# FFN gate and up projections: one 512-column matmul for the upper weight part, halves added when PSUM is read

## The chip, the cores and the metric

The kernel runs on one core of a Trainium2 chip. The metric is the device time of one execution in microseconds (us); the number given for a kernel is the median of its runs. All data are float32; a matmul operand is tagged float32r.

## What is computed

Two layers of a hybrid trunk act on x of 256 tokens by 1024 channels. Each layer is an FFN, a block of three token mixers, and a second FFN, each followed by a residual and a LayerNorm. The change touches the FFNs alone; there are four of them.

```python
D_MODEL = 1024
SEQ = 256
DEPTH = 2
D_FF = 2816

def _swiglu(x, w_in, w_out):
    gate, up = jnp.split(x @ w_in, 2, axis=-1)
    return (jax.nn.silu(gate) * up) @ w_out

def reference(...):
    for l in range(DEPTH):
        x = _layernorm(DEEPNORM_ALPHA * x + FFN_RES * _swiglu(x, ffn1_w_in[l], ffn1_w_out[l]),
                       ln1_g[l], ln1_b[l])
        mix = _hybrid_mixer(x, l, ...)
        x = _layernorm(DEEPNORM_ALPHA * x + mix, ln2_g[l], ln2_b[l])
        x = _layernorm(DEEPNORM_ALPHA * x + FFN_RES * _swiglu(x, ffn2_w_in[l], ffn2_w_out[l]),
                       ln3_g[l], ln3_b[l])
    return x
```

## The kernel before

**Split products.** Every float32 operand of a matmul is held as two parts: an upper part (hi, a copy rounded to float32r) and a lower part (lo, what is left). A product a·b is three matmuls into the same PSUM region, hi·hi, hi·lo and lo·hi (`passes`, line 124). Weights come from HBM by SP's queue into `raw` (`wraw`, 2 buffers of 1 MB; `rawo` for the output weights); ScalarE makes `whi` (L93) and VectorE subtracts to make `wlo` (L94), in pieces of 128x1024 out of the pool `wsp`, which has 6 buffers of each. `split_act` (L128, L129) does the same to activations. In the trace PE names the stationary operand second: `gm<-xThi,whi` has weights `whi` loaded and `xThi` streamed through.

**Activations.** `new_xT` allots two tiles of 128 x (8·256 + 128) elements, `xThi` and `xTlo`, and uses 8·256 columns of each from column `APART` = 48 (192 bytes) on. `transposed` fills them after each LayerNorm (L145, L128, L129). Both the FFNs and the mixers read them.

**One FFN** (`ffn`, line 236) walks over 11 blocks of 256 hidden channels, j = 0 to 10.
- Block 0 is done by `part_a` with tokens as output rows (L275), so that it can begin with the first half of the tokens while the second half still goes through the LayerNorm before.
- Blocks 1 to 10 are done by `part_s`: two weight loads (gate and up, 1 MB each), then `gemm_s` (L135) four times: gate f=0 and f=1 into the two halves of one PSUM tile `pg`, up f=0 and f=1 into those of `pu`. A `gemm_s` is 8 steps k of three matmuls, each with 256 columns of x streamed. ScalarE applies Silu to `pg` (L297), VectorE multiplies by `pu` (L300), and `split_act` makes `hhi` and `hlo`.
- `out_mm` (L308) multiplies h of block j−2 (`LAG` = 2) by its output weights, 24 matmuls of 512 columns into four PSUM accumulators that stay open for the whole FFN. The second token half of the last three blocks is held back (`HOLD` = 3) to cover the LayerNorm of the first half.

**PSUM.** The pools `gm` and `tp` have two banks each, `at` has four. `pg` and `pu` are the two `gm` banks; `tp` serves transposes.

**Order.** Each engine runs its instructions in the order in which a scheduler that simulates the program wrote them down; an engine waits where the next one in its list is not ready.

**Mixers.** Between the FFNs stand projections of the same split kind: `block_s`, `gate` and `proj` through `gemm_s` (also L135, 256 columns), `block_a` (L368, 512 columns of weights streamed, x loaded as the stationary operand), and `mix_out` (L730).

Of the kernel before, what the change touches and what calls it, by code (L numbers as in the profile page):

```python
# [11 lines left out]
F32 = mybir.dt.float32  # L12
F32R = mybir.dt.float32r
BF16 = mybir.dt.bfloat16
AF = mybir.ActivationFunctionType
# [5 lines left out]
P = 128  # L21
D = 1024
S = 256
L = 2
FF = 2816
KT = D // P
# [4 lines left out]
HOLD = 3  # L31

APART = 48
OFF_QA, OFF_KA, OFF_VA, OFF_ZB, OFF_XBC, OFF_DTB, OFF_QC, OFF_KC, OFF_VC, OFF_G = (
    0, 1024, 2048, 3072, 4096, 5632, 5648, 6672, 7696, 8720)
NEG = -float(2 ** 100)
# [4 lines left out]
def hybrid_trunk(ctx: ExitStack, tc: tile.TileContext, x, ffn1_w_in, ffn1_w_out, ln1_g, ln1_b,  # L41
# [4 lines left out]
    pe, act, dve, pool = nc.tensor, nc.scalar, nc.vector, nc.gpsimd  # L46

    const = ctx.enter_context(tc.tile_pool(name="const", bufs=1))
    keep = ctx.enter_context(tc.tile_pool(name="keep", bufs=1))
# [8 lines left out]
    def gm_tile():  # L58
        return gm.tile([P, 512], F32, name="gm")

    def tp_tile():
        return tp.tile([P, 512], F32, name="tp")
# [48 lines left out]
    def load_cols(w, c0, between=None, raw=None):  # L111
        return load(w, 0, 8, c0, 256, None, between, raw)
# [4 lines left out]
    def load_block(w, c0):  # L117
        return load_half(w, 0, c0) + load_half(w, 4, c0)
# [5 lines left out]
    def passes(a, b):  # L124
        return ((a[0], b[0]), (a[0], b[1]), (a[1], b[0]))

    def split_act(hi, lo, src):
        act.copy(out=hi, in_=src)  # L128
        dve.tensor_sub(out=lo, in0=src, in1=hi.bitcast(F32))  # L129

    def gemm_s(ps_out, w, f, xT, n=P):
        first = True
        for k in range(KT):
            for i, (a, b) in enumerate(passes(w[k], xT)):
                pe.matmul(out=ps_out, lhsT=a[:, f:f + n], rhs=b[:, k, :],  # L135
                          start=first, stop=(k == KT - 1 and i == 2))
                first = False


    def transposed(t, xT):  # L140
        for q in range(2):
            pt = tp_tile()
            for i in range(4):
                k = 4 * q + i
                pe.transpose(out=pt[:, i * P:(i + 1) * P], in_=xt[:, t, k * P:(k + 1) * P], identity=ident)  # L145
            pv = pt.rearrange("p (k c) -> p k c", c=P)
            split_act(xT[0][:, 4 * q:4 * q + 4, t * P:(t + 1) * P], xT[1][:, 4 * q:4 * q + 4, t * P:(t + 1) * P], pv)

    def new_xT():
        def part(name):  # L150
            whole = keep.tile([P, KT * S + 128], F32R, name=name)
            return whole[:, APART:APART + KT * S].rearrange("p (k c) -> p k c", c=S)

        return part("xThi"), part("xTlo")

    def layernorm(t, accs, coef, gb, sq):
        st = sm.tile([P, 5], F32, name="st")
# [78 lines left out]
    def ffn(xT, w_in, w_out, g, b, l, pre, prefetch, fresh=False, last=False, tiles_a=1):  # L236
        NJ = FF // 256
        with tc.tile_pool(name="ffn", bufs=2, reuse_waits="tile") as fp:
# [7 lines left out]
            def new_h():  # L246
                return (fp.tile([P, 2, S], F32R, name="hhi", bufs=5), fp.tile([P, 2, S], F32R, name="hlo", bufs=5))
# [40 lines left out]
            def part_s(j):  # L288
                spare = fresh and j == 1
                wg = load_cols(w_in[l], j * 256, None, raws[0] if spare else None)  # L290
                wu = load_cols(w_in[l], FF + j * 256, None, raws[1] if spare else None)
                pg, pu = gm_tile(), gm_tile()
                hT = new_h()
                for f in range(2):
                    gemm_s(pg[:, f * S:(f + 1) * S], wg, f * P, xT)
                sg = fp.tile([P, 512], F32, name="h")
                act.activation(out=sg, in_=pg, func=AF.Silu)  # L297
                for f in range(2):
                    gemm_s(pu[:, f * S:(f + 1) * S], wu, f * P, xT)
                dve.tensor_mul(out=sg, in0=sg, in1=pu)  # L300
                split_act(hT[0], hT[1], sg.rearrange("p (f c) -> p f c", c=S))
                return hT

# [10 lines left out]
            for j in range(tiles_a, NJ + LAG):  # L314
                if j < NJ:
                    hs[j] = part_s(j)
                pj = j - LAG
                if pj < 0:
                    continue
                if pj < NJ - HOLD:  # L320
                    wo = load_rows(w_out[l], 2 * pj, None, raws[pj] if pj < 2 and not fresh else new_raw())
                    for t in range(NT):
                        out_mm(pj, hs[pj], wo, t)
                else:
                    wo = load_rows(w_out[l], 2 * pj, held_pair(), new_raw())
                    if pj < NJ - 1:
                        out_mm(pj, hs[pj], wo, 0)
                    else:
                        pre2 = prefetch and prefetch()
                        for h in range(2):  # L330
                            out_mm(pj, hs[pj], wo, 0, (h,))
                    held.append((pj, wo))
                if pj == NJ // 2:
                    load_gb(gb, g, b, l)
                if fresh and pj == 2:
                    consts.append(mixer_constants())
            for t in range(NT):
                if t == 1:
                    for h in range(2):
                        for pj, wo in held:  # L340
                            out_mm(pj, hs[pj], wo, 1, (h,))
                layernorm(t, accs[t], 0.5, gb, sq)
                if last:
                    for h in range(2):
                        nc.sync.dma_start(out=out_v[:, t, 512 * h:512 * h + 512], in_=xt[:, t, 512 * h:512 * h + 512])
                else:
                    if xT2 is None:
                        xT2 = new_xT()
                    transposed(t, xT2)
# [3 lines left out]
    def mixer(xT, l, pre, prefetch, consts):  # L353
# [4 lines left out]
        with tc.tile_pool(name="mix", bufs=1, reuse_waits="tile") as mp:  # L358
            def slot(tag, shape, dt=F32):
                return mp.tile(shape, dt, name=tag, tag=tag)  # L360
# [17 lines left out]

            ss = mp.tile([P, APART], F32, name="ss")[:, 0:2 * 8].rearrange("p (t h) -> p t h", h=8)
            zs = slot("t1", [P, NT, D])  # L380
# [383 lines left out]
            for t in range(NT):  # L764
                if t == 1:
                    for h in range(2):
                        for q in (1, 2, 3):
                            mix_out(q, wo[q], t, (h,))
                layernorm(t, accs[t], 0.5, gb, slot("xde", [P, D]))
                if xT2 is None:  # L770
                    xT2 = new_xT()
                transposed(t, xT2)
        return xT2, pre2

    def ffn_first(w_in, l, between=None):
        return lambda: (load_cols(w_in[l], 0, between), load_cols(w_in[l], FF))

    xT = new_xT()
    consts = []
    pre = ffn_first(ffn1_w_in, 0, lambda: load_x(0, 1))()  # L780
    for l in range(L):
        xT, pre = ffn(xT, ffn1_w_in, ffn1_w_out, ln1_g, ln1_b, l, pre, lambda: load_block(w_mix_in[l], OFF_ZB),
                      fresh=(l == 0))
        xT, pre = mixer(xT, l, pre, ffn_first(ffn2_w_in, l), consts[0])
        last = l == L - 1
        xT, pre = ffn(xT, ffn2_w_in, ffn2_w_out, ln3_g, ln3_b, l, pre, None if last else ffn_first(ffn1_w_in, l + 1), last=last)
# [37 lines left out]
```

## Time and profile before

| | us |
|---|---|
| median of 3 runs | 1610.74 |
| lowest and highest run | 1610.71, 1612.2 |
| the profiled execution, its own time | 1617.37 |
| its span, first to last instruction | 1615.6 |
| TensorE (PE) busy in the span | 1591.5 (99%) |
| VectorE (DVE) busy | 984.7 (61%) |
| ScalarE (ACT) busy | 848.4 (53%) |
| mean granted TensorE clock, share of full speed | 0.994 |

PE's busy time does not say how fast it goes: matmuls overlap, and a row's duration (282 ns for a 256-column one) is longer than the distance from its start to the next one's start. How long a stretch of matmuls takes is read from the chain of work that ended last, which lists stretches of one engine and one line with start, length and count. The profiled execution took 6.63 us more than the median of the runs; sums are made on its rows and carried over as differences.

### The profile page before, as it was taken

Reading aid. Unit: us, or ns where it says so; the run is one execution under the profiler, and the core shown is the slowest. Engines: PE = TensorE matmul, PEld = TensorE weight load, DVE = VectorE, ACT = ScalarE, POOL = GpSimd, SP = SyncE. Lnnn points to the kernel's source line nnn. Section 1 sums busy time; section 2 is a strip of 40 time slices with the busy share of each in tenths; the row PEclk is TensorE's granted clock in tenths of the full one; section 3 lists DMA queues with packets and bytes.
Section 4 is the critical chain, followed back from the end, with each engine's and each line's share of the span. In section 5 each row is a group of like instructions: output and inputs, shape, how many; then the busy total and the mean of one; then the engine's idle time right before and its main releaser. Section 6 shows DMA issues by size and latency. Waiting matters only on the chain.

```text
span 1615.6 us, 26930 instructions
## 1 busy us (share of the span) xinstructions
PE 1591.5 (99%) x11282; PEld 1467.2 (91%) x11282; DVE 984.7 (61%) x1510; ACT 848.4 (53%) x1285; POOL 17.6 (1%) x28
## 2 busy tenths in 40 slices
PE   8999999999999999999999999999999999999998
PEld 8999899888799998999899998998788999999997
DVE  5555657767585556455655565777576855565454
ACT  5545356568675444444444453654676755444451
POOL 0000000000000000000000000000000000000000
PEclk9999999999999999999999999998999999999999
DMA  8665445543435674566445562663443356545651
GB/s 286 198 226 192 158 157 175 187 161 105 157 106 174 217 235 140 175 216 225 157 162 203 209 230 85 208 190 128 154 140 124 129 194 216 191 157 183 235 196 39
DMA packets 222117, 283.55 MB, mean 176 GB/s; under 512 B 8658, under 2 KB 185644, under 8 KB 221996
## 3 DMA queue, kind: packets, MB, share of 16 engines
q1 hardware_dynamic: 213676, 277.61, 51.0%
q10 hardware_dynamic: 8320, 4.23, 0.9%
q8 instruction: 88, 1.44, 0.4%
q14 instruction: 33, 0.27, 0.0%
HBM read 280.74 MB, written 1.08 MB: 174 GB/s over the span
## 4 chain that ended last, share of the span: by engine, by line
PE 95%; DVE 2%; DMA 2%; ACT 1%; issue 0%; POOL 0%; DVEq 0%; POOLq 0%; ACTq 0%
PE gm L135 52%; PE at L308 15%; PE gm L368 14%; PE gm L275 3%; PE at L730 2%; DMA t<-acd 2%; PE at L633 1%; PE at L507 1%; PE at L585 1%; PE at L577 1%; PE at L555 1%; PE tp L614 0%; DVE wlo L94 0%; DVE at L169 0%; DVE xt L160 0%; PE tp L145 0%
## 5 line engine op out<-in xcount | busy, mean ns | idle before, releaser
L94 DVE TENSOR_TENSOR wlo<-raw,whi 128x1024 fp32r<-128x1024 f32 x412 | 501.2, 1223 | 360.5 <-ACT whi L93 350.4
L93 ACT CAST whi<-raw 128x1024 fp32r<-128x1024 f32 x412 | 429.4, 1051 | 391.0 <-PE gm L135 229.4
L135 PE MATMUL gm<-xThi,whi 128*128 128x256 f32 x2112 | 595.1, 282 | 0.0
L135 PE MATMUL gm<-xTlo,whi 128*128 128x256 f32 x2112 | 594.8, 282 | 0.0
L135 PE MATMUL gm<-xThi,wlo 128*128 128x256 f32 x2112 | 594.2, 281 | 0.0
L135 PEld LDWEIGHTS gm<-xThi,wlo 128*128 128x128 f32 x2112 | 403.8, 191 | 1.8 <-issue 1.8
L135 PEld LDWEIGHTS gm<-xThi,whi 128*128 128x128 f32 x2112 | 398.4, 189 | 3.4 <-issue 1.8
L135 PEld LDWEIGHTS gm<-xTlo,whi 128*128 128x128 f32 x2112 | 397.9, 188 | 3.0 <-issue 1.6
L135 PE MATMUL gm<-t,whi 128*128 128x256 f32 x768 | 138.7, 282 | 0.0
L368 PE MATMUL gm<-whi,xThi 128*128 128x512 f32 x320 | 128.7, 402 | 1.2 <-ACT xThi L128 1.2
L94 DVE TENSOR_TENSOR wlo<-rawo,whi 128x1024 fp32r<-128x1024 f32 x68 | 83.1, 1225 | 72.8 <-ACT whi L93 69.7
L368 PE MATMUL gm<-whi,xTlo 128*128 128x512 f32 x320 | 126.9, 398 | 0.0
L368 PE MATMUL gm<-wlo,xThi 128*128 128x512 f32 x320 | 126.4, 395 | 0.0
L135 PEld LDWEIGHTS gm<-t,whi 128*128 128x128 f32 x768 | 117.2, 188 | 2.7 <-issue 2.7
L93 ACT CAST whi<-rawo 128x1024 fp32r<-128x1024 f32 x68 | 71.3, 1052 | 76.8 <-PE at L308 63.7
L135 PE MATMUL gm<-t,wlo 128*128 128x256 f32 x384 | 108.1, 281 | 0.0
L308 PE MATMUL at<-whi,hhi 128*128 128x512 f32 x256 | 78.9, 390 | 0.0
L308 PE MATMUL at<-wlo,hhi 128*128 128x512 f32 x256 | 78.9, 390 | 0.0
L308 PE MATMUL at<-whi,hlo 128*128 128x512 f32 x256 | 78.9, 390 | 0.0
L135 PEld LDWEIGHTS gm<-t,wlo 128*128 128x128 f32 x384 | 73.1, 190 | 0.0
L368 PEld LDWEIGHTS gm<-whi,xThi 128*128 128x128 f32 x320 | 60.3, 188 | 13.9 <-ACT xThi L128 2.1
L368 PEld LDWEIGHTS gm<-whi,xTlo 128*128 128x128 f32 x320 | 60.2, 188 | 13.5 <-DVE xTlo L129 0.9
(235 smaller groups left out, 1870.5 us busy)
## 6 DMA issues: line engine op xcount, KB each, us to landing
raw<-in_w_mix_in_dram SPq DMA_DIRECT2D x92, 1024.0 KB, 5.1
raw<-in_ffn_w_in_dram SPq DMA_DIRECT2D x85, 1024.0 KB, 4.9
rawo<-in_ffn_w_out_dram SPq DMA_DIRECT2D x44, 1024.0 KB, 7.2
raw<-in_w_branch_dram SPq DMA_DIRECT2D x24, 1024.0 KB, 5.5
raw<-in_w_mix_out_dram SPq DMA_DIRECT2D x8, 1024.0 KB, 6.2
t<-acd ACTq DMA_DIRECT2D x4, 1024.0 KB
rawo<-in_ffn_w_in_dram SPq DMA_DIRECT2D x2, 1024.0 KB
gb<-in_ln_g_dram SPq DMA_DIRECT2D x4, 512.0 KB
```

The lines of the kernel that those rows point to most:

```text
L93: act.copy(out=hi, in_=src)
L94: dve.tensor_sub(out=lo, in0=src, in1=hi.bitcast(F32))
L135: pe.matmul(out=ps_out, lhsT=a[:, f:f + n], rhs=b[:, k, :], start=first, stop=(k == KT - 1 and i == 2))
L275: pe.matmul(out=ps[:, u * 256:(u + 1) * 256], lhsT=a[:, k, t * P:(t + 1) * P], rhs=c, start=first, stop=(k == KT - 1 and i == 2))
L308: pe.matmul(out=accs[t][h], lhsT=a[:, f, t * P:(t + 1) * P], rhs=c[:, h * 512:(h + 1) * 512], start=(j == 0 and f == 0 and i == 0), stop=( ...
L368: pe.matmul(out=ps, lhsT=a[:, k, t * P:(t + 1) * P], rhs=c, start=(k == 0 and i == 0), stop=(k == KT - 1 and i == 2))
L507: pe.matmul(out=py[:, 64 * h:64 * h + 64], lhsT=m[:, hh, :], rhs=xdt[:, c, 64 * hh:64 * hh + 64], start=True, stop=True)
L555: pe.matmul(out=pz[h][:, 0:S], lhsT=kcT[r, hp, 0:P], rhs=qcT[r, hp, :], start=True, stop=False, skip_group_check=True)
L577: pe.matmul(out=pz[h][:, 0:384], lhsT=trin, rhs=part[:, hs], start=False, stop=False, skip_group_check=True)
L585: pe.matmul(out=pz[c0][64 * h:64 * h + 64, 384:512], lhsT=vct[:, k, 64 * hh:64 * hh + 64], rhs=sp[:, 384 * h + c1:384 * h + c1 + P], start ...
L633: pe.matmul(out=pm[m][:, c:c + n], lhsT=qaT[r, h, t * P:(t + 1) * P], rhs=kaT[r, h, 0:n], start=True, stop=True, skip_group_check=True)
L730: pe.matmul(out=accs[t][h], lhsT=a[:, k, t * P:(t + 1) * P], rhs=c[:, h * 512:(h + 1) * 512], start=(k == 0 and i == 0), stop=(k == KT - 1 ...
```

## The change

- `new_xT` allots one tile of 128 x (8·512 + 128) elements. For each k it holds 256 columns of the upper part and, right behind, 256 of the lower one. It returns the two parts as before (now strided) and, as a third item, the whole with 512 columns per k. The data begin at column `XPART` = 48, 192 bytes.
- `gemm_j` takes the place of `gemm_s` in `part_s`. For each k it issues one matmul of 512 columns (upper weights by both parts of x) and one of 256 (lower weights by the upper part of x, added to columns 0 to 255). Three matmuls and three weight loads per k become two and two.
- The result of one f fills a whole PSUM bank: columns 256 to 511 hold hi·lo, columns 0 to 255 the rest. ScalarE copies the upper half to SBUF and VectorE adds the lower half to it, for each of the four products of a block. Silu and the multiplication then read SBUF. Gate uses the two `gm` banks, up the two `tp` banks.
- The mixers and `part_a` keep their instructions and read x from the new places.

```diff
+XPART = 48
...
+    def gemm_j(w, f, xT, ps):
+        for k in range(KT):
+            pe.matmul(out=ps, lhsT=w[k][0][:, f:f + P], rhs=xT[2][:, k, :], start=(k == 0), stop=(k == KT - 1),
+                      skip_group_check=True)
+            pe.matmul(out=ps[:, 0:S], lhsT=w[k][1][:, f:f + P], rhs=xT[0][:, k, :], start=False, stop=(k == KT - 1),
+                      skip_group_check=True)
+        return ps
...
     def new_xT():
-        def part(name):
-            whole = keep.tile([P, KT * S + 128], F32R, name=name)
-            return whole[:, APART:APART + KT * S].rearrange("p (k c) -> p k c", c=S)
-
-        return part("xThi"), part("xTlo")
+        whole = keep.tile([P, KT * 2 * S + 128], F32R, name="xTj")[:, XPART:XPART + KT * 2 * S]
+        both = whole.rearrange("p (k i c) -> p k i c", i=2, c=S)
+        return both[:, :, 0, :], both[:, :, 1, :], whole.rearrange("p (k c) -> p k c", c=2 * S)
...
-                pg, pu = gm_tile(), gm_tile()
                 hT = new_h()
+                sg = fp.tile([P, 512], F32, name="h")
                 for f in range(2):
-                    gemm_s(pg[:, f * S:(f + 1) * S], wg, f * P, xT)
-                sg = fp.tile([P, 512], F32, name="h")
-                act.activation(out=sg, in_=pg, func=AF.Silu)
+                    ps = gemm_j(wg, f * P, xT, gm_tile())
+                    sf = sg[:, f * S:(f + 1) * S]
+                    act.copy(out=sf, in_=ps[:, S:2 * S])
+                    dve.tensor_add(out=sf, in0=sf, in1=ps[:, 0:S])
+                act.activation(out=sg, in_=sg, func=AF.Silu)
+                su = fp.tile([P, 512], F32, name="h")
                 for f in range(2):
-                    gemm_s(pu[:, f * S:(f + 1) * S], wu, f * P, xT)
-                dve.tensor_mul(out=sg, in0=sg, in1=pu)
+                    ps = gemm_j(wu, f * P, xT, tp_tile())
+                    sf = su[:, f * S:(f + 1) * S]
+                    act.copy(out=sf, in_=ps[:, S:2 * S])
+                    dve.tensor_add(out=sf, in0=sf, in1=ps[:, 0:S])
+                dve.tensor_mul(out=sg, in0=sg, in1=su)
```

How the instructions move is shown at three places. **First, PE inside a gate block.** In the kernel before, two steps k of one product read as follows; `gm` is the PSUM tile.

```order
L135 MATMUL gm<-xThi,whi 128x256
L135 MATMUL gm<-xTlo,whi 128x256
L135 MATMUL gm<-xThi,wlo 128x256
L135 MATMUL gm<-xThi,whi 128x256
L135 MATMUL gm<-xTlo,whi 128x256
L135 MATMUL gm<-xThi,wlo 128x256
```

In the changed kernel the same work on PE is the following, where `xTj` is the joint tile; L143 and L145 are the two matmuls of `gemm_j`.

```order
L143 MATMUL gm<-xTj,whi 128x512
L145 MATMUL gm<-xTj,wlo 128x256
L143 MATMUL gm<-xTj,whi 128x512
L145 MATMUL gm<-xTj,wlo 128x256
L143 MATMUL gm<-xTj,whi 128x512
```

Sixty-four such matmuls stand where 96 stood in each of the blocks 1 to 10, and the 24 of `out_mm` follow them as before.

**Second, ScalarE over one block of the first FFN.** Before, its list has one Silu from PSUM (L297), the upper parts of six weight pieces (L93) and that of h (L128).

```order
L93 CAST whi<-raw 128x1024 x2
L297 ACTIVATE h<-gm 128x512
L93 CAST whi<-raw 128x1024 x2
L128 CAST hhi<-h 128x512
L93 CAST whi<-rawo 128x1024 x2
```

In the changed kernel four copies from PSUM are among them (L305 for gate, L312 for up; L95, L130 and L307 are the casts and the Silu).

```order
L305 COPY h<-gm 128x256
L95 CAST whi<-raw 128x1024 x2
L305 COPY h<-gm 128x256
L312 COPY h<-tp 128x256
L307 ACTIVATE h<-h 128x512
L95 CAST whi<-raw 128x1024 x2
L312 COPY h<-tp 128x256
L130 CAST hhi<-h 128x512
L95 CAST whi<-rawo 128x1024 x2
```

VectorE's list changes in the same way: four additions (L306, L313) stand between its subtractions for the weights.

**Third, PE where the second layer's first FFN begins**, behind the first token half of block 0. Before, transposes of the second token half (L145) stand among the last matmuls of `part_a`.

```order
L145 MATMUL tp<-ident,xt 128x128 x4
L275 MATMUL gm<-whi,xThi 128x256
L275 MATMUL gm<-wlo,xThi 128x256
L145 MATMUL tp<-ident,xt 128x128 x4
L275 MATMUL gm<-whi,xTlo 128x256
```

In the changed kernel all eight transposes (L155) come after the first half's 48 matmuls, and those of h (L291) follow after two more of `part_a` (L283 there).

```order
L155 MATMUL tp<-ident,xt 128x128 x8
L283 MATMUL gm<-whi,xTj 128x256
L283 MATMUL gm<-wlo,xTj 128x256
L291 MATMUL tp<-ident,h 128x128 x2
L283 MATMUL gm<-whi,xTj 128x256 x2
```

The first products of block 1 are also mixed in among the rest of `part_a` there. In the mixers PE's order is the same as before, and so is the order of the transfers on SP's queue.

## Rows read from the trace of the kernel before

**Rows 1.** The page's part 1: busy us (share of span) xinstructions; and the chain's shares.
```profile
PE 1591.5 (99%) x11282; PEld 1467.2 (91%) x11282; DVE 984.7 (61%) x1510; ACT 848.4 (53%) x1285; POOL 17.6 (1%) x28
...
PE 95%; DVE 2%; DMA 2%; ACT 1%; issue 0%; POOL 0%; DVEq 0%; POOLq 0%; ACTq 0%
PE gm L135 52%; PE at L308 15%; PE gm L368 14%; PE gm L275 3%; PE at L730 2%; DMA t<-acd 2%; PE at L633 1%; PE at L507 1%; PE at L585 1%; PE at L577 1%; PE at L555 1%; PE tp L614 0%; DVE wlo L94 0%; DVE at L169 0%; DVE xt L160 0%; PE tp L145 0%
```

**Rows 2.** What PE waited for, whole span: us in total, times, longest us.
```profile
PE tp L145 <- DMA xt<-in_x_dram: 5.4, 2, 4.6
PE gm L275 <- DVE xTlo L129: 3.7, 4, 1.6
PE at L507 <- DVE t L501: 3.1, 2, 1.6
```

**Rows 3.** Chain, steady stretch of the third FFN: start us, length us, what, xmatmuls.
```profile
882.35 11.31 PE gm L135 x96
893.66 5.44 PE at L308 x24
899.10 11.31 PE gm L135 x96
910.40 5.44 PE at L308 x24
```

**Rows 4.** Chain where gate blocks of FFNs 1, 2 and 4 begin.
```profile
22.58 4.33 PE gm L135 x38
...
632.16 3.75 PE gm L135 x33
...
1434.80 3.75 PE gm L135 x33
```

**Rows 5.** Chain in the first mixer block.
```profile
204.35 16.77 PE gm L368 x72
...
222.94 13.38 PE gm L135 x118
...
522.92 57.95 PE gm L135 x492
```

**Rows 6.** Groups by line and form: xcount | busy us, mean ns | idle before, releaser.
```profile
L297 ACT ACTIVATE h<-gm 128x512 f32<-128x512 f32 x40 | 23.5, 589 | 6.5 <-PE gm L135 6.5
L425 ACT ACTIVATE w<-w 128x512 f32<-128x512 f32 x8 | 5.0, 626 | 0.0
L279 ACT ACTIVATE h<-gm 128x256 f32<-128x256 f32 x8 | 3.1, 384 | 3.1 <-PE gm L275 3.1
L128 ACT CAST hhi<-tp 128x256 fp32r<-128x256 f32 x8 | 2.9, 368 | 8.1 <-PE tp L283 8.1
...
L280 DVE TENSOR_TENSOR h<-h,gm 128x256 f32<-128x256 f32 x8 | 3.3, 416 | 0.6 <-ACT h L279 0.5
```

**Rows 7.** One block's stretch: us, then busy of PE, PEld, DVE, ACT, POOL; clock, DMA.
```profile
893.66:910.40 16.74, 16.74 (x121) 15.81 (x121) 8.45 (x9) 7.43 (x9) 0.00 (x0) 1.00 0.70 253
```

**Rows 8.** ACT and DVE in that stretch: start us, length, what [idle before, releaser].
```profile
903.30 1.05 ACT L93 CAST whi<-raw 128x1024 fp32r<-128x1024 f32 x1 [3.06 <-PE gm L135]
904.73 1.05 ACT L93 CAST whi<-raw 128x1024 fp32r<-128x1024 f32 x1 [0.37 <-PE gm L135]
...
905.81 1.23 DVE L94 TENSOR_TENSOR wlo<-raw,whi 128x1024 fp32r<-128x1024 f32 x1 [0.20 <-ACT whi L93]
```

**Rows 9.** Chain from the second to the third FFN.
```profile
788.83 16.34 PE at L308 x72
...
808.93 3.90 PE gm L275 x31
812.84 0.45 PE tp L145 x4
...
813.93 0.70 DVE xTlo L129
...
814.67 3.45 PE gm L275 x27
```

## The prediction

> **What bounds the kernel now.** Read first the busy times and the shares of the chain of work that ended last [rows 1]: PE is busy for 99% of the span and holds 95% of the chain, and 52 points of those are line L135, which the change rewrites for the FFNs. Then read what PE waits for [rows 2]: a first load of x, and single waits at LayerNorms; none stands inside the gate and up blocks. So in those blocks the end is set by how fast PE issues matmuls. That is not in their durations but in the chain in order of time [rows 3]: 96 matmuls of 256 columns take 11.31 us, 117.8 ns each from start to start, and the 24 of 512 columns between them take 5.44 us, 226.7 ns each. The stretches adjoin without a gap (893.66 + 5.44 = 899.10), so switching width costs nothing that shows. Two 256-column matmuls take 235.6 ns and one of 512 takes 226.7: 8.9 ns less for the same columns. That is what the change can win; the columns streamed stay the same.
>
> **The change part by part.**
>
> *The merged matmuls.* `part_s` runs for 10 blocks in each of 4 FFNs, with 4 products of 8 steps: 1280 steps. A step was 3 · 117.8 = 353.4 ns. It becomes a 512 and a 256. Neither alternates with the other singly anywhere before, so both prices are bounded. For the 512 the low end is 226.7 [rows 3]; the high end is the slowest steady stretch of that width, 72 in 16.77 us, 232.9 ns, where x is loaded and weights are streamed [rows 5]. For the 256 the high end is 117.8; the low end is a stretch of the same line in the mixers, 118 in 13.38 us, 113.4 ns [rows 5]. Best: 226.7 + 113.4 = 340.1, a gain of 13.3 ns a step, 17.0 us in all. Worst: 232.9 + 117.8 = 350.7, a gain of 2.7, or 3.5 us. I take 226.7 + 117.8 = 344.5, since these stand side by side in the FFN itself, with the same weight buffers and the same x, and the 256s keep 117.8 directly behind a 512: a gain of 8.9 ns, 11.4 us. The exception is the beginning of block 1 in three FFNs, 38 + 33 + 33 matmuls at 113.6 to 113.9 [rows 4]. There a step already takes about 341 ns, so some 35 steps win nothing: 0.3 us off. Sum of this part: −11.1 us.
>
> *The copies and additions.* Four times a block ScalarE copies 128x256 out of PSUM and VectorE adds 128x256. The nearest rows for the copy are 368 and 384 ns; the addition has the very form of the 416 ns row [rows 6]. Silu of 512 columns from SBUF takes 626 ns in place of 589. So ACT gets 4 · 0.38 + 0.04 = 1.6 us more in a block and DVE 4 · 0.42 = 1.7. In a block of 16.74 us they are busy for 7.43 and 8.45 [rows 7], so they come to 9.0 and 10.1 of a new 16.45. I cost them at nothing because their queues run ahead. The gate weights of the next block are cast at 903.30 and 904.73, as soon as PE releases their buffers; their lower parts are done at 905.81 + 1.23 = 907.04 [rows 8]; PE reads them at 910.40 + 5.44 = 915.84 [rows 3], 8.8 us later. If that cover went, a late piece would stop PE for as long as it is late. The banks are no limit either: each of the four is written once a block, so it has some 13 us to be emptied.
>
> *The last block.* h of block 10 is ready later by a copy and an addition, 0.8 us. Its way out of PSUM was a multiplication, a cast and a subtraction, about 2 us, and becomes about 3. In front of its own `out_mm` stand 24 matmuls of blocks 8 and 9, a third of the 72 in 16.34 us [rows 9], 5.4 us. Covered.
>
> *Order at the LayerNorms.* Between FFN 2 and 3 PE stands from 813.29 to 814.67 for xTlo [rows 9]. The transposes now come 3 matmuls later (0.35 us), and two transposes of h move into this wait. Both signs are possible, half a microsecond each at three places; taken as zero.
>
> *The joint tile.* Mixers and `part_a` read x with the same instructions from other places. What that does to their pitch no row can show, as the trace holds only one layout. Bounds: 52% of the span, 840 us, is L135; 40 · 11.31 = 452 of it lies in the FFNs, leaving 388 in the mixers. Of these, 2 · 57.95 already go at 117.8 (492 in 57.95 us, once in each layer) [rows 5]. The other 272 could rise by at most 117.8/113.4, 10.6 us, and if the 388 all came down to 113.4 from 117.8, that would give 14.5. I take zero, since the mixers show both pitches with one layout, so the places alone don't decide it.
>
> **Sum:** −11.1 us. The profiled execution of 1617.37 would become 1606.3; it lies 6.6 above the median, and the median of 1610.7 becomes **1599.6 us**.
>
> **The rivals.**
>
> *The 256 speeds up too.* The first product of block 1 runs at 113.4 to 113.9 [rows 4], so the fast pitch exists in the FFN. If the slack of the 512 in front lets each 256 run so, the gain is 17.0 − 0.3: **1594.0**. Against it: behind every `out_mm` the 256s are at 117.8 from the first [rows 3]. Chance 0.13.
>
> *The 512 is dear.* If x streamed in 512 columns costs 229 to 233 ns as streamed weights do in the mixers [rows 5], the gain is 3.5 to 8 us: **1605**. For it: same width, same engine. Against it: 226.7 in the FFN. Chance 0.16.
>
> *Nothing per instruction.* At the fast pitch two 256s are 2 · 113.4 = 226.8, exactly one 512: a matmul costs by the column there, and the 4.4 ns more in the FFN may belong to the state of the gate block and not to an instruction. Then the 512 carries it twice, a step stays at 353.4, and the time stays at **1610.7**. Against it: `out_mm` doesn't carry it, and the 512 leaves more time for the next weight load than a 256. Chance 0.13. [...]
>
> *The joint layout reads worse (the slower side).* The two reads of PE, streamed x and loaded weights, may get into each other's way more when the parts lie in one tile. The price: up to 10.6 us in the mixers, and 512s of 232.9 ns in the FFN that leave only 3.5 of the gain: 1610.7 + 10.6 − 3.5 = **1617.8** at worst. It decides as soon as the mixers lose more than the FFNs win: 11.1 at my price, 3.5 at the worst one. For it: the spread of pitches in [rows 5]. Against it: both pitches at one layout. Chance 0.09. With it goes a smaller one: an addition that waits for its product holds back a weight subtraction behind it on DVE. To come out slower that must stop PE by over 14.3/40 = 0.36 us in each block, out of a lead of 8.8; chance 0.03.
>
> **How the numbers follow.** My forecast (gain 8 to 14 us) has 0.46. A difference under 0.2%, 3.2 us, is what a measurement of this kernel can't tell from none. Faster takes the forecast, the quick 256 and the dear 512: 0.46 + 0.13 + 0.16 = 0.75. Same is the rival with nothing per instruction, 0.13; slower 0.12. The range goes from the quick 256, **1593**, to **1608**, which takes in the dear 512 whole and the edge of no gain; it leaves out the slower side and most of no gain, some 0.2.
>
> **What would show it.** In the chain of the changed kernel a block's 64 matmuls of L143 and L145 should take 32 · 344.5 = 11.02 us in place of 11.31, with `out_mm` still at 5.44, so a block's period is 16.46. At 10.88 the 256s have sped up; at 11.2 the 512s are dear; at 11.31 nothing is won per instruction. PE's waits should show no new line for the weights or PSUM in the FFNs. The mixers' 492 matmuls should again take 57.95 us, and the 118 at 222.94 again 13.38; other numbers there are the layout's doing. PE should count 1280 matmuls less, ACT and DVE some 64 and 67 us more. The forecast is wrong if a block's 64 matmuls take 11.2 us or more, if a wait for `whi`, `wlo` or a PSUM tile appears in every block, or if the mixers move by more than 3 us.

## The result, and the profile after

The changed kernel took 1621.11 us (median of 8 runs, 1615.68 to 1623.54), the kernel before beside it 1610.72 (8 runs, 1609.73 to 1613.96): a ratio of 1.0053, 95% interval 1.0035 to 1.0071. It is slower by half a per cent, where 1599.6 was forecast. Two later repeats gave smaller ratios, 1.0019 (1.0000 to 1.0039) and 1.0027 (1.0008 to 1.0045). The profiled execution after is the quickest of its eight, 1615.68 us with a span of 1613.9; that of before, 1617.37, lies above all of its timed runs. So the two spans alone would say the opposite of the verdict, and the traces are compared stretch by stretch.

The page after, part 1 and the chain's shares, against [rows 1]:

```profile
PE 1590.3 (99%) x10002; PEld 1403.9 (87%) x10002; DVE 1051.8 (65%) x1670; ACT 903.2 (56%) x1447; POOL 17.6 (1%) x28
...
PE gm L137 24%; PE at L322 15%; PE gm L382 14%; PE tp L143 9%; PE gm L143 9%; PE gm L145 5%; PE tp L145 5%; PE gm L283 3%; PE at L744 2%; DMA t<-acd 1%; PE at L647 1%; PE at L599 1%; PE at L521 1%; PE at L591 1%; PE at L569 1%; PE tp L628 0
```

There are 1280 matmuls fewer, as foreseen, and 63 us less of weight loading, but PE is busy for as long as before. What held 52% of the chain as L135 is now 24% in the mixers (L137) and 28% in the new lines L143 and L145.

What PE waited for after, whole span (us in total, times, longest us), against [rows 2]:

```profile
PE tp L155 <- DMA xt<-in_x_dram: 6.5, 2, 3.6
PE gm L283 <- DVE xTj L131: 3.5, 3, 1.6
PE gm L283 <- ACT xTj L130: 2.3, 4, 0.9
PE at L521 <- DVE t L515: 2.1, 1, 2.1
```

No line names `whi`, `wlo` or a PSUM tile of the gate and up products. The evacuation, four copies and four additions a block, makes PE wait nowhere.

The chain after in the third FFN (start us, length us, what), against [rows 3]:

```profile
886.95 0.23 PE gm L143
887.18 0.12 PE gm L145
887.30 0.23 PE gm L143
...
898.25 5.47 PE at L322 x24
903.72 0.23 PE gm L143
```

This is the reading that decides. The block's 64 matmuls run from 886.95 to 898.25: 11.30 us, where 96 took 11.31. By the recorded starts, over 1280 steps, the 256 follows its 512 after 235.0 ns and the next 512 follows after 118.0 (medians). The pair is 353 ns, the old step of 3 · 117.8. `out_mm` is 0.03 us longer than in [rows 3], and a block's period is 16.77 us (886.95 to 903.72) instead of 16.74.

PE's timeline where block 1 of the first FFN begins (start us, duration us, instruction), against [rows 4]:

```profile
23.10 0.39 PE L143 MATMUL gm<-xTj,whi 128*128 128x512 f32 x1
23.33 0.28 PE L145 MATMUL gm<-xTj,wlo 128*128 128x256 f32 x1
...
23.80 0.40 PE L143 MATMUL gm<-xTj,whi 128*128 128x512 f32 x1
```

From 23.10 to 23.80 two pairs take 0.70 us: here too, where single 256s had gone at 113.6 to 113.9 ns, a pair now costs some 350. The durations, 390 and 280 ns, again say nothing of the pitch.

The chain after in the first mixer block, against [rows 5]:

```profile
204.88 16.77 PE gm L382 x72
...
223.48 13.38 PE gm L137 x118
...
527.32 57.95 PE gm L137 x492
```

Groups of the evacuation after (xcount | busy us, mean ns | idle before, releaser), against [rows 6], and one block's window (us, then busy of PE, PEld, DVE, ACT, POOL; clock, DMA share, GB/s), against [rows 7]:

```profile
L313 DVE TENSOR_TENSOR h<-h,tp 128x256 f32<-128x256 f32 x80 | 33.3, 416 | 27.1 <-ACT h L312 27.0
...
L305 ACT COPY h<-gm 128x256 f32<-128x256 f32 x80 | 29.5, 369 | 51.8 <-PE gm L145 51.5
...
L307 ACT ACTIVATE h<-h 128x512 f32<-128x512 f32 x40 | 25.4, 634 | 3.3 <-DVE h L306 3.3
```

```profile
886.95:903.72 16.77, 16.77 (x89) 14.32 (x89) 10.24 (x13) 8.75 (x12) 0.00 (x0) 1.00 0.55 190
```

The mixers' stretches are the old ones to the last digit. Additions, copies and Silu cost what the nearest rows said (416, 369 and 634 ns), and DVE and ACT fill 10.24 and 8.75 us of a block.

**Where do the 10 us come from, if the blocks changed by 0.03?** From the granted clock. Each layer of the changed kernel has the same stretch of its mixer behind a transfer of 12 us. Here is the chain for both layers, and under it the two windows:

```profile
281.04 12.06 DMA t<-acd
...
296.17 4.76 PE at L521 x32
300.93 4.91 PE gm L137 x23
...
1081.55 11.51 DMA t<-acd
...
1096.12 3.79 PE at L521 x32
1099.91 2.67 PE gm L137 x23
```

```profile
296.17:305.84 9.67, 9.67 (x57) 9.67 (x58) 9.67 (x16) 3.63 (x4) 0.00 (x0) 0.65 0.33 108
1096.12:1102.58 6.46, 6.46 (x57) 6.46 (x58) 6.46 (x12) 4.30 (x5) 0.00 (x0) 1.00 0.10 21
```

The same 55 matmuls took 9.67 us in one layer and 6.46 in the other. In the first the mean granted clock is 0.65, and from 299 to 305 us it is 0.50, half speed; in the second it is 1.00 throughout. Ahead of the first PE had stood for 2.1 us (L521 in the waits above); ahead of the second its products reached until the data were there. But the standstill alone doesn't decide it: in another execution of the changed kernel (a_again below) PE stood 2.16 us at the first place and ran on at full speed (clock 1.00 from 290 to 310 us), as its chain shows:

```profile
295.81 3.79 PE at L521 x32
299.59 2.77 PE gm L137 x23
```

The kernel before has such stretches too, in the second layer's mixer (clock 0.50 from 1095 to 1104 us) and behind the LayerNorm ahead of its last FFN (its windows, same columns):

```profile
1080.00:1100.00 20.00, 18.41 (x138) 18.21 (x137) 15.80 (x41) 11.59 (x13) 0.00 (x0) 0.85 0.63 191
1100.00:1120.00 20.00, 20.00 (x140) 18.64 (x140) 15.84 (x23) 7.66 (x14) 1.02 (x1) 0.90 0.43 144
...
1420.00:1440.00 20.00, 19.16 (x151) 19.16 (x152) 11.89 (x18) 7.65 (x13) 0.56 (x1) 0.91 0.41 138
```

They come and go from run to run of one kernel, and each run lists its mean clock. Over 98 runs of the kernel before (one more, with an odd clock of 0.946, is left out) it lies between 0.990 and 0.999, and the time goes with it: 1608.04 at 0.999, 1622.03 at 0.990. A line through the 26 runs of the first series with clocks falls by 1.64 us per 0.001, one through all 98 by 1.55. So in what follows each kernel also has a time **at clock 0.995**: the mean of its runs, each moved by 1.65 us per 0.001, an estimate from that first series. By that the kernel before stands at 1615.0 to 1615.6 in five series, and the changed one at 1617.0, 1617.3 and 1616.9 in its three. The change itself costs about 1.8 us. The first comparison's runs of the changed kernel had a mean clock of 0.9929, its lowest series; those of the kernel before list none, but by the same 1.65 us a median of 1610.72 would belong to some 0.9977. On this estimate, which takes the clock from the time itself, the difference of 0.0048 is 7.9 us: with the 1.8, 9.7 of the measured 10.4.

### The profile page after: what moved, and what is told of

Its sections match the earlier page's. It is cut to its first block, busy times and chain, and to the rows that moved or that the text cites. A ratio compares the mean times of both kernels' runs of the same rounds, so it can differ in the third digit from the quotient of the medians.

```text
span 1613.9 us, 24767 instructions
## 1 busy us (share of the span) xinstructions
PE 1590.3 (99%) x10002; PEld 1403.9 (87%) x10002; DVE 1051.8 (65%) x1670; ACT 903.2 (56%) x1447; POOL 17.6 (1%) x28
## 4 chain that ended last, share of the span: by engine, by line
PE 95%; DVE 2%; DMA 2%; ACT 0%; issue 0%; POOL 0%; SPq 0%; DVEq 0%; POOLq 0%; ACTq 0%
PE gm L137 24%; PE at L322 15%; PE gm L382 14%; PE tp L143 9%; PE gm L143 9%; PE gm L145 5%; PE tp L145 5%; PE gm L283 3%; PE at L744 2%; DMA t<-acd 1%; PE at L647 1%; PE at L599 1%; PE at L521 1%; PE at L591 1%; PE at L569 1%; PE tp L628 0%
## 5 line engine op out<-in xcount | busy, mean ns | idle before, releaser
L95 ACT CAST whi<-raw 128x1024 fp32r<-128x1024 f32 x412 | 429.8, 1051 | 257.5 <-PE gm L137 112.6
L137 PE MATMUL gm<-xTj,whi 128*128 128x256 f32 x1664 | 297.7, 281 | 0.0
L137 PEld LDWEIGHTS gm<-xTj,whi 128*128 128x128 f32 x1664 | 255.4, 189 | 3.9 <-issue 3.4
L137 PE MATMUL gm<-xTj,wlo 128*128 128x256 f32 x832 | 233.5, 281 | 0.0
L143 PE MATMUL gm<-xTj,whi 128*128 128x512 f32 x640 | 228.3, 397 | 0.0
L143 PE MATMUL tp<-xTj,whi 128*128 128x512 f32 x640 | 228.0, 397 | 0.0
L382 PE MATMUL gm<-whi,xTj 128*128 128x512 f32 x640 | 209.5, 399 | 0.7 <-ACT xTj L130 0.7
L145 PE MATMUL gm<-xTj,wlo 128*128 128x256 f32 x640 | 179.9, 281 | 0.0
L145 PE MATMUL tp<-xTj,wlo 128*128 128x256 f32 x640 | 179.8, 281 | 0.0
L137 PEld LDWEIGHTS gm<-xTj,wlo 128*128 128x128 f32 x832 | 158.2, 190 | 1.8 <-issue 1.8
L143 PEld LDWEIGHTS tp<-xTj,whi 128*128 128x128 f32 x640 | 120.3, 188 | 29.8
L143 PEld LDWEIGHTS gm<-xTj,whi 128*128 128x128 f32 x640 | 120.3, 188 | 28.8
L382 PEld LDWEIGHTS gm<-whi,xTj 128*128 128x128 f32 x640 | 119.1, 188 | 27.1 <-ACT xTj L130 1.7
L137 PE MATMUL gm<-t,whi 128*128 128x256 f32 x768 | 138.6, 281 | 0.0
L382 PE MATMUL gm<-wlo,xTj 128*128 128x512 f32 x320 | 126.3, 395 | 0.0
L145 PEld LDWEIGHTS gm<-xTj,wlo 128*128 128x128 f32 x640 | 120.2, 188 | 1.2
L145 PEld LDWEIGHTS tp<-xTj,wlo 128*128 128x128 f32 x640 | 120.1, 188 | 0.0
L137 PEld LDWEIGHTS gm<-t,whi 128*128 128x128 f32 x768 | 117.2, 188 | 2.7 <-issue 2.7
L137 PE MATMUL gm<-t,wlo 128*128 128x256 f32 x384 | 107.9, 281 | 0.0
L95 ACT CAST whi<-rawo 128x1024 fp32r<-128x1024 f32 x68 | 71.5, 1054 | 18.0 <-PE at L322 14.2
```

The lines of the kernel that those rows point to most:

```text
L137: pe.matmul(out=ps_out, lhsT=a[:, f:f + n], rhs=b[:, k, :], start=first, stop=(k == KT - 1 and i == 2))
L143: pe.matmul(out=ps, lhsT=w[k][0][:, f:f + P], rhs=xT[2][:, k, :], start=(k == 0), stop=(k == KT - 1), skip_group_check=True)
L145: pe.matmul(out=ps[:, 0:S], lhsT=w[k][1][:, f:f + P], rhs=xT[0][:, k, :], start=False, stop=(k == KT - 1), skip_group_check=True)
L382: pe.matmul(out=ps, lhsT=a[:, k, t * P:(t + 1) * P], rhs=c, start=(k == 0 and i == 0), stop=(k == KT - 1 and i == 2))
```

## The experiments

The question was twofold: what had kept a step at 353 ns (a fixed price of the step, the joint tile, the place of x, or the order of the two widths), and whether the surplus was the change's own or the clock's. All ratios are to the kernel before on the same chip.

| label | edit | median us (runs) | ratio, 95% interval | mean clock | at 0.995 | block period, FFN 3 |
|---|---|---|---|---|---|---|
| b_again | the kernel before | 1614.71 (10) | 1.0004, 0.9981 to 1.0027 | 0.9950 | 1615.0 | 16.74 |
| a_again | the changed kernel | 1618.85 (10) | 1.0019, 1.0000 to 1.0039 | 0.9949 | 1617.3 | 16.77 |
| layout | joint tile alone | 1612.33 (10) | 1.0003, 0.9983 to 1.0023 | 0.9961 | 1615.5 | 16.74 |
| x0 | x at byte 0 | 1623.49 (5) | 1.0061, 1.0038 to 1.0084 | 0.9954 | 1623.5 | 16.80 |
| x16 | x at byte 64 | 1616.67 (8) | 1.0002, 0.9978 to 1.0026 | 0.9970 | 1620.5 | 16.64 |
| x32 | x at byte 128 | 1618.83 (8) | 1.0031, 1.0008 to 1.0054 | 0.9968 | 1622.1 | 16.66 |
| x64 | x at byte 256 | 1620.38 (8) | 1.0040, 1.0013 to 1.0066 | 0.9971 | 1624.2 | 16.79 |
| rel2 | weights 192 bytes further on | 1624.25 (3) | 1.0061, 1.0027 to 1.0096 | 0.9950 | 1624.0 | 16.80 |
| grouped | eight 512s, then eight 256s | 1610.00 (8) | 0.9969, 0.9945 to 0.9992 | 0.9940 | 1607.3 | 16.56 |
| bgroup | before, three runs of eight by kind | 1608.67 (4) | 0.9966, 0.9934 to 0.9998 | 0.9980 | 1613.8 | 16.74 |
| bgroup2 | the same, `block_a` too | 1612.08 (8) | 0.9993, 0.9978 to 1.0008 | 0.9964 | 1614.6 | 16.75 |
| grouped_all | grouped, mixers' `gemm_s` too | 1607.42 (3) | 0.9946, 0.9910 to 0.9983 | 0.9940 | 1606.9 | 16.56 |
| a_third | the changed kernel | 1616.61 (12) | 1.0027, 1.0008 to 1.0045 | 0.9949 | 1616.9 | 16.77 |
| grouped_again | grouped | 1609.05 (12) | 0.9973, 0.9956 to 0.9991 | 0.9941 | 1607.4 | 16.56 |

### Both kernels again

No edit in either.

> The kernel before, unchanged, for a second trace and the granted clock of each run. Theory C (the clock): its runs at 1610 to 1612 us go with a mean granted clock of about 0.997, above the 0.994 of the profiled 1617.37 us, and the time falls by about 2 us for each 0.001 of clock. Theory D (rival: the changed kernel has slower instructions that its profiled run happened not to show): the clock does not go with the time. Blocks of 96 matmuls again take 11.31 us by either.

> The changed kernel, unchanged, for a second trace. Theory C: 1616 to 1624 us, a mean granted clock of 0.991 to 0.995, stretches at half clock that add up to more than in the kernel before, at a place where PE had stood still; a block's 64 matmuls again take about 11.30 us. Theory D: the clock is the same as in the kernel before, and the stretch that is longer is in the FFN blocks or the mixers at full clock.

The kernel before spread over 1609.41 to 1623.16 us, against 1609.73 to 1613.96 in the first comparison: the first 8 runs had shown too little of its spread. The changed kernel's ratio fell from 1.0053 to 1.0019, while its block stayed at 16.77 us, its mixers at 13.38 and 57.95. The time goes with the clock, by 1.64 us per 0.001 in the 26 runs of the kernel before, where some 2 were expected. The trace of a_again shows one stretch of lowered clock ahead of the end (0.70 from 620 to 625 us) where that of the first run showed two (0.50 from 300 to 305, 0.83 from 620 to 630), and the two traces of the kernel before show three (0.72 from 620 to 625, 0.50 from 1095 to 1100, 0.66 from 1420 to 1425) and two (0.50 from 300 to 305, 0.83 from 620 to 630); so the expectation that the changed kernel has more of them isn't borne out by the traces. The pitches belong to the kernel; most of the headline belongs to the clock that a run was granted.

### The joint tile alone

```diff
-                    ps = gemm_j(wg, f * P, xT, gm_tile())
+                    gemm_s(pg[:, f * S:(f + 1) * S], wg, f * P, xT)
...
-                    ps = gemm_j(wu, f * P, xT, tp_tile())
+                    gemm_s(pu[:, f * S:(f + 1) * S], wu, f * P, xT)
```

`part_s` is as in the kernel before, so the copies and additions are left out along with the merged matmul.

> The joint tile alone: part_s as in the kernel before, three matmuls of 256 columns, no copies and additions, but x read from the joint tile. Theory L (the layout makes x slower to read): 1618 to 1622 us, as the whole change. Theory M (what costs comes with the merged matmuls, copies and additions): 1609 to 1613 us, as the kernel before, blocks of 96 in 11.31 us.

The chain of layout (start us, length us, what):

```profile
892.01 5.44 PE at L316 x24
908.75 5.44 PE at L316 x24
```

A period of 16.74 us, the 118 in 13.38, the 492 in 57.95, `out_mm` at 5.44: every stretch is that of the kernel before, and so is the time (1.0003). The layout costs nothing and gains nothing. The 0.03 us of `out_mm` came with the merged matmul or with the copies and additions; no run parts the two. Its profiled execution, too, shows the clock's part: PE stood for 0.94 us ahead of the mixer's stretch and ran on at full speed, a clock of 1.00 from 280 to 320 us (PE's timeline of layout):

```profile
294.57 0.66 PE L515 MATMUL at<-t,t 128*128 128x64 f32 x4 [0.94 <-DVE t L509]
```

### The place of x

```diff
-XPART = 48
+XPART = 0
```

and 16, 32 and 64 in the same line (elements of 4 bytes).

> The changed kernel with the joint tile's data at byte 0 and not 192. Theory A (the 512-column matmul's 235 ns against out_mm's 227 ns comes from where x lies): another pitch than 235 ns in L143, 227 ns if the place is the whole cause, then about 10 us less than the changed kernel. Theory S (it is a state of the run of matmuls, not a place): 235 ns again, time as the changed kernel within 4 us.

> The joint tile's data at byte 64. With byte 0 the mixers' 118 matmuls took 14.16 us and with 192 13.38, the gate block's pair 352.0 ns and 353.4. Theory A (place against the loaded weights): 118 matmuls between or outside these, and a pair that differs from 353 ns by more than 2. Theory S (a state of the gate block whatever the place): the pair within 2 ns of 353.

> The joint tile's data at byte 128. Theory A: a pair that differs from 353 ns by more than 2, and another time for the mixers' 118 matmuls than 13.38 us. Theory S: the pair within 2 ns of 353.

> The joint tile's data at byte 256. If only the place within some power of two up to 256 bytes matters, as byte 0: 118 matmuls in about 14.16 us, pair about 352 ns. If the place within a larger unit matters, other numbers.

The chain of x0, then that of x16:

```profile
222.84 14.16 PE gm L137 x118
...
530.82 57.43 PE gm L137 x492
...
885.84 5.50 PE at L322 x24
902.64 5.50 PE at L322 x24
```

```profile
203.97 17.07 PE gm L382 x72
...
882.65 5.47 PE at L322 x24
899.29 5.47 PE at L322 x24
```

The mean distances of the two starts were 235.3 and 116.7 ns in x0 and in x64 (pair 352.0), 230.6 and 119.0 in x16 (349.6), 230.6 and 120.0 in x32 (350.6). Three things follow. Bytes 0 and 256 read alike in every stretch: the 118 in 14.16 us, the 492 in 57.43 and `out_mm` in 5.50 in both, the 72 of L382 in 16.61 and 16.64; no other two places 256 bytes apart were run. The 512 and the 256 shift against each other by up to 5 ns while their sum stays within 349.6 to 353 ns, at most 4 ns under the 353.4 of the kernel before (what three 256s take at these places was not run). And the place sets the mixers as well: against the changed kernel x16 wins 3.5 ns a step, 4.5 us in 1280, and loses more elsewhere. Summed by recorded starts, its 960 matmuls of L382 take 3.5 us more, and its 2496 of L137 on x a mean of 1.9 ns, 4.8 us, more. At equal clock it is the slower kernel, though its ratio of 1.0002 looks the better one: its mean clock was 0.9970.

Neither theory held whole at byte 0: the 512s stayed at a mean of 235, yet the time rose by 6.5 us at equal clock. Theory A held at byte 128 (the 118 in 14.00 us); at byte 64 the pair differed by 3.8 ns, but the 118 stayed at 13.38.

### The place of the weights

```diff
-        whole = keep.tile([P, KT * 2 * S + 128], F32R, name="xTj")[:, XPART:XPART + KT * 2 * S]
+        whole = keep.tile([P, KT * 2 * S + 128 + XPART], F32R, name="xTj")[:, XPART:XPART + KT * 2 * S]
```

x keeps byte 192 of its 256; everything allotted behind its tile, the weights among it, moves there too from byte 0.

> The changed kernel with 192 bytes of padding behind the joint tile, so that the weight buffers lie 192 bytes further on: x stays where it was, and x and weights come to the same place within 256 bytes, as they do with the joint tile's data at byte 0. Theory R (the place of x against the weights decides the pitch): the numbers of byte 0, 118 matmuls of the mixers in 14.16 us, L143 mostly at 232 and 240 ns, the time 6 us above the changed kernel at the same clock. Theory B (x's own place decides): 13.38 us, L143 at 235, the changed kernel's time.

The chain of rel2:

```profile
223.09 14.22 PE gm L137 x118
...
884.71 5.50 PE at L322 x24
901.51 5.50 PE at L322 x24
```

14.22 and 5.50 us, a period of 16.80 and pitches of 236.0 and 116.8 ns: the stretches of x0, whose x and weights also stand alike. The 512s of both spread, mostly from 230 to 241 ns, where those of the changed kernel are nearly all at 235. What counted in these runs is therefore not where x lies by itself but how it lies to the weights. Having them apart by 192 bytes, as both kernels of this study do, was worth 7 us to the changed one at equal clock (1624.0 against 1617.0).

It isn't slower everywhere, and it reaches matmuls that don't read x. In the 492 (57.95 us in the changed kernel, 57.43 in x0) products on x take turns with products on the mixers' outputs (tile `t`). By recorded starts those on x rise there from 117.8 to 119.7 ns in x0, and those on `t` fall from 117.8 to 113.9, though neither `t` nor the weights have moved. L382, where x is loaded, falls too (x0):

```profile
204.38 16.61 PE gm L382 x72
```

So the pitch of the products on `t` moved with what ran beside them; how, these runs don't show.

### The order of the two widths

```diff
         for k in range(KT):
             pe.matmul(out=ps, lhsT=w[k][0][:, f:f + P], rhs=xT[2][:, k, :], start=(k == 0), stop=(k == KT - 1),
                       skip_group_check=True)
+        for k in range(KT):
             pe.matmul(out=ps[:, 0:S], lhsT=w[k][1][:, f:f + P], rhs=xT[0][:, k, :], start=False, stop=(k == KT - 1),
```

> gemm_j with its 8 matmuls of 512 columns first and its 8 of 256 columns behind. Theory P (the surplus is paid by the streamed column of x in this block): 512s at 235 ns also in a run, 256s at 118, a product 8 * 353 = 2.83 us as in the changed kernel, the time within 3 us at the same clock. Theory N (it comes from single alternation of the two widths): 512s fall to 227 ns, a block is shorter by 32 * 8 ns = 0.26 us, and the time by about 10 us.

> The grouped form of gemm_j (eight 512s, then eight 256s) once more beside the changed kernel, for an interval. If what it won is pitch (2.775 in place of 2.83 us a product, 160 products: 8.8 us) it stands at a ratio of 0.993 to 0.997 to the kernel before whatever clock it draws, and below the changed kernel by 8 to 12 us. If it won by a lucky clock, the ratio is 0.999 to 1.003. The 512s should again go at 232 to 233 ns and the 256s at 114.

The chain of grouped_again in the third FFN:

```profile
875.81 5.46 PE at L323 x24
881.26 1.86 PE gm L143 x8
883.13 0.92 PE gm L146 x8
...
891.46 0.91 PE tp L146 x8
892.37 5.46 PE at L323 x24
```

In groups the 512s take 232.5 ns (1.86 us for eight) and the 256s 114. The block's 64 matmuls go from 881.26 to 892.37, 11.11 us in place of 11.30, and the period falls to 16.56: 40 · 0.18 = 7.2 us against the kernel before. At clock 0.995 it is 7.8 below it and 9.6 below the changed kernel. Both series are under the kernel before by their whole interval, with a mean clock that is lower than that one's, so it is pitch that won. **This version beats both.** The ratio of 0.9973 misses the expected 0.993 to 0.997 by a hair, and so do the 7.6 us between the medians of grouped_again and a_third, for 8 to 12; at equal clock these two are 9.4 us apart. Neither of the prices first expected of grouped held: the 512s came down by little, and the gain is mostly the 256s, which went at 114 ns in runs of eight.

### Grouping without merging

```diff
-        first = True
-        for k in range(KT):
-            for i, (a, b) in enumerate(passes(w[k], xT)):
+        for i in range(3):
+            for k in range(KT):
+                a, b = passes(w[k], xT)[i]
```

in the kernel before (bgroup); the same in `block_a`'s loop (bgroup2); and in the mixers' `gemm_s` of grouped (grouped_all).

> The kernel before with the three kinds of product each in a run of 8 in gemm_s (all k of hi by hi, then lo of x, then lo of the weights), no merging, no joint tile. Theory O (the order of the loads and streams sets the pitch, as grouping did for the changed kernel, where the 256s fell from 118 to 114 ns): a block's 96 matmuls in 10.9 us (113.5 ns each) and the mixers' 492 in about 55.9 us, the time 1585 to 1600 us. Theory N (grouping helps the merged form alone): 11.31 and 57.95 us, the time as before.

> As the one before, and block_a's 24 matmuls of 512 columns (L368 of the kernel before) also in runs of 8 by kind. Theory O: 72 of them in 16.3 us (227 ns) in place of 16.77. Theory N: 16.77 us again, or more.

> The changed kernel with gemm_j grouped as before, and gemm_s of the mixers in runs of 8 by kind too. Theory O: FFN products at 2.78 us as grouped, and the mixers' 492 in about 55.9 us; 5 to 8 us less than grouped alone at the same clock. Theory N: the mixers as in the changed kernel.

The chain of bgroup:

```profile
530.11 50.57 PE gm L135 x446
...
586.17 10.91 PE gm L135 x96
...
891.26 5.44 PE at L307 x24
908.00 5.44 PE at L307 x24
```

In the FFN grouping by kind alone moves nothing: 16.74 us, as theory N has it. So the order helped there only where two widths alternated (11.30 us a block to 11.11). In the mixers theory O holds: the stretch that was 492 in 57.95 us goes at 446 in 50.57, 113.4 ns each in place of 117.8, and the 96 at 586 take 10.91 us, 113.6 ns each, for 11.31. So 256s alone, all reading the same places as before, went at either pitch here, by their order. The time as a whole shows little of it. bgroup's good ratio is its clock, 0.9980; at 0.995 it is 1.4 us below the kernel before on 4 runs, and bgroup2 0.6, where theory O had at least 10. Summed by recorded starts, with breaks and half-speed stretches left out, L135 takes 4 to 5 us less; what took most of it back was not traced. In grouped_all the same two stretches gain as much, but the whole is within 0.5 us of grouped. In bgroup2 the matmuls of `block_a`, by recorded starts, take a mean of 233 ns as before, not the 227 of theory O.

### Is the lower clock the change's doing?

No edit.

> The changed kernel once more, to tell where the larger part of its headline comes from. At equal granted clock it has so far been some 1.8 us above the kernel before; the rest of the first result's 10 us went with its mean granted clock, 0.9940 over 18 runs against 0.9957 over 26 of the kernel before, at about 1.65 us per 0.001. Theory C (the changed kernel itself brings on a lower clock): its mean clock is again at least 0.0015 below that of the kernel before on the same chip, and the ratio is 1.0025 to 1.005. Theory D (the clock is drawn run by run, whatever the kernel): the mean clocks lie within 0.001 of each other, the ratio is 0.9995 to 1.0025. In both the pitches are as before: 235 and 118 ns, a block's 64 matmuls in 11.3 us.

The mean clocks were 0.9949 against 0.9964, the ratio 1.0027: by the numbers set beforehand this is theory C, at its very edge. Over all series the changed kernel has 0.9944 (30 runs) and the kernel before 0.9959 (98 runs). But the 30 hold the first 8, which raised the question; the other 22 have 0.9949, 0.0010 lower with a standard error of 0.0004. So the changed kernel probably draws a lower clock, by 0.0010 to 0.0015, which is 1.6 to 2.5 us; this is not shown beyond doubt. With the 1.8 at equal clock it makes some 3.4 to 4.3 us, a ratio of 1.0021 to 1.0027, near those of the two later series. The rest of the first headline would then be the scatter of the draw. Why the clock is lower isn't settled. At each LayerNorm ahead of a second FFN PE stands for 0.94 and 1.62 us in every profiled run of every kernel here, yet half speed followed in some runs and not in others: behind the first of the two places the clock was 0.50 from 625 to 630 us in a_third, in layout it was 1.00 behind both. PE's standstill ahead of the first layer's L521 differs: 2.13 to 2.16 us in the three profiled runs of the changed kernel, 1.48 and 1.66 in the two of the kernel before. Its length alone is no rule either: a_again ran on at 1.00 behind 2.16 us, and x0 and x32 fell to a mean of 0.66 behind 1.32 and 1.20 (from 300 to 310 us). Against a rule by the kind of matmul stand x16 and x32, with merged matmuls and clocks of 0.9970 and 0.9968.

## Why the prediction was wrong

**The step that failed** is the price of the 512: "I take 226.7 + 117.8 = 344.5, since these stand side by side in the FFN itself, with the same weight buffers and the same x". The reason given is false: `out_mm` reads no x at all. It is a stretch in which 512 follows 512, and the roles are the other way round, with h loaded (named second) and the output weights streamed:

```profile
893.50 0.62 PE L308 MATMUL at<-whi,hhi 128*128 128x512 f32 x2
```

Singly between 256s, with weights loaded and x streamed, a 512 took 235.0, and the sum stayed at 353 ns. The term of −11.4 us measured nothing (11.30 us a block in place of 11.31). The bounds failed with it: both prices of a 512, 226.7 and 232.9, came from streamed weights and from pure stretches, so 232.9 was no upper end and the sum could only come out as a gain. That "switching width costs nothing that shows" was read where the width changes twice a block, not at every matmul. x16 and grouped show that prices near 231 to 233 exist for this very matmul, so with x and weights 192 bytes apart the alternation itself cost 2 ns on the 512 and 4 on the 256, 6 of the 8.9 ns that were forecast for a step. The 6 ns by which a grouped 512 stays above `out_mm`'s were not traced: no run swapped the loaded and the streamed operand, or grouped at another place of x.

**The rival that happened** is "nothing per instruction": 11.31 us was its mark, and the block measured 11.30. Its own reason, that the 4.4 ns are the gate block's and the 512 carries them twice, fits the 235 (two 256s at 117.8 are 235.6). But grouped takes 6 ns off the pair by order alone, and rel2 shifts the two prices against each other, so "the state of the block" comes down at least to the order of the widths and to how x lies to the weights. What happens inside PE stays open. Against three 256s a step won 0 ns with the widths alternating (11.30 us a block for 11.31) and about 6 with them grouped (11.11).

**The exception at block 1** was counted as "some 35 steps win nothing". They lost: the 104 fast matmuls of [rows 4] now cost the common 353 a step, about 4 ns more each, 0.4 us. The matmuls of `out_mm`, summed by recorded starts, take 240.37 us in place of 239.23, 1.1 more; together that is 1.5 of the 1.8 us at equal clock. The rest was not traced.

**The copies and additions** were right in size (on DVE and ACT 10.1 and 9.0 us a block were forecast, 10.24 and 8.75 measured; over the whole run 67 and 64 us more, 67.1 and 54.8 measured) and in their cover: PE waits for none of them. **The joint tile** was right at zero: 13.38, 57.95 and 16.77 us again, and layout at 1.0003. The slower rival, that the joint layout reads worse, is refuted by that run, though the result has its sign. **The last block and the LayerNorms** show no new wait of any size.

**The range and the median.** "The median of 1610.7 becomes 1599.6" took three runs that agreed within 1.5 us for the kernel's spread. It has 14 us of it, by the clock. Even a right sum could have been read off by 4 us, as the kernel before's own median moved from 1610.74 to 1614.71, and no part of the range held that.

## What to carry to other kernels

Take a matmul's price from a stretch in which it has the same neighbours and the same operand loaded, not from a pure run of its width: merging two 256-column matmuls into one of 512 saved nothing here as long as it alternated with 256s, and 8 us once equal widths stood together. Where the price comes from another place in the program, let the bounds reach to no gain at all. And where differences are below half a per cent, read each run's granted clock beside its time, and compare kernels at equal clock or by the length of one undisturbed block.

## What the runs showed of the hardware

- A matmul's pitch here moved with how its streamed operand lay to the loaded one. With x and weights both at byte 0 (x0), both at 192 (rel2), and x at 256 with the weights at 0 (x64), the 118 of the mixers took 14.16, 14.22 and 14.16 us; with x 64, 128 and 192 bytes from the weights (x16, x32, the changed kernel) 13.38, 14.00 and 13.38. It also moved with the matmuls beside it: products on `t` went from 117.8 to 113.9 ns when x alone was moved (x0).
- With x and weights 192 bytes apart, a 256-column matmul of `gemm_j` went at 114 ns among its like behind a run of 512s, and at 118 singly behind a 512; a 512 at 232.5 and 235 ns. Among 256s alone both pitches occurred: ordered by kind (bgroup) they went at 117.8 ns in the FFN, 96 in 11.31 us, and in the mixers that order moved a stretch from 117.8 to 113.4.
- The same program, the kernel before, was granted a mean clock between 0.990 and 0.999 of full speed from run to run, 14 us on 1610. The half-speed stretches looked at (clock 0.50) lay behind places where PE stood still: 55 matmuls took 9.67 us behind 2.13 us of standing, and 6.46 where it had not stood. But the same standstill was followed by half speed in one run and by full speed in another: the 55 took 6.56 us in a_again, behind 2.16 us, and behind the LayerNorms (0.94 and 1.62 us) the clock went to 0.50 in a_third and stayed at 1.00 in layout.
